# V tiles of two dilations and the combined products kept in DRAM per head pair, in rows of 8 KB

## The chip, the cores and the metric

The kernel runs on one core of a Trainium2 chip. A core has a matrix engine (TensorE, in the profile PE, with its weight loads PEld), a vector engine (DVE), a scalar engine (ACT), GpSimd (POOL) and a queue engine (SP). Each executes its own instructions in order and waits on semaphores for the others. Transfers between DRAM and the on-chip memory (SBUF) are carried out by 16 DMA engines; an instruction of SP, ACT or POOL issues them. The metric is device time in microseconds of one execution, the median of several runs. Before the change it is 2009.21 us.

## The reference

One decoder layer: a projection of `x` (2048 positions x 1024) to queries, keys, values, gates and the inputs of a state-space mixer; causal attention with three dilations; the mixer; a norm for each branch; one output projection; a residual and a layer norm. Cut to the part that the change touches:

```python
DILATIONS = (1, 4, 16)                       # 16 heads of 64, 128 steps back
for o, l in dilation 1, 4, 16: o, l = dilated_window_attention(q, k, v, slopes, dilation)
wts = softmax(stack([l1, l2, l3]))
y_att = wts[0] * o1 + wts[1] * o2 + wts[2] * o3
y_att = rms_norm(y_att * silu(z_att), att_norm_g)
...
mix = concatenate([y_att, y_ssm])
x = layer_norm(alpha * x + mix @ w_out, ln_g, ln_b)
```

In the kernel the heads go in pairs (`pr`, 0 to 7): a pair is one row of 128 channels. The kernel counts the dilations backwards: `d` = 0 is dilation 16, `d` = 1 is 4, `d` = 2 is 1.

## The kernel before, in words

**First stage, about 0 to 1150 us.** The input projection, as fast matrix products of 7 instead of 8 blocks, runs as 37 jobs. PE works through job after job (L260 to L264, L309), while ACT, DVE and POOL prepare the weights of the next one: ACT rounds a block to the high half (L216), POOL or DVE forms the low half (L217). Into this stream are put the convolution, from about 1/3 of the stage, and the 32 units of the state-space mixer, in the last third. The order of PE, DVE, ACT and POOL is that of the program (a manual schedule); `after(n, f)` puts `f` n steps later, a step being one of the 7 products of a job.

Four jobs give the values. `fin_v` (L353) stores them to `d_v[0]`, an array of [16, 128, 1024] floats whose rows, 4 KB each, are one position with all heads. `copy_v(s, b)` (L547), issued by POOL, then makes a second array `d_v[1]` with the positions in the order of dilation 4: for each of the two column halves `s`, 16 copies of 128 rows of 2 KB, from step 95 (first half) and step 254 (second).

**Second stage, attention, about 1150 to 1610 us.** Eight pairs, each with 3 dilations x 4 quarters x 2 halves = 24 units. A unit is: scores on PE (L947), a reduction with the bias table on DVE (L953), exponentials on ACT (L962), transposes on PE (L976, L984) that DVE copies out (L978, L987), and the products with V on PE (L1002). V of one dilation is a tile `v` of 128 partitions x 16 blocks x 128 channels, and, for `d` > 0, a second tile `vs` with the same rows moved by 64. `load_v` (L880) fetches them: `d` = 0 from `d_v[0]` by four POOL transfers; `d` = 1 from `d_v[1]` by POOL; `d` = 2 from `d_v[0]`, for all pairs but the first by SP. In all of these, one row of a transfer is the 128 channels of one pair at one position: 512 bytes. The order of SP's queue is the program's too in this stage.

After the last unit of a pair its softmax statistics are written to `d_st`, gathered again in another layout (`cm`, L1061), and made into the weights of the three dilations by DVE, ACT and POOL (`weights`, L1063). The weights are stored to `d_wd` (L1081) and broadcast to 64 partitions per head (`broadcast`, L1083, tiles `wb`), while PE is already at the next pair. `broadcast` begins, for `d` > 0, with a DVE memset of one element of the tile (L1087). POOL multiplies and adds (`combine`, L1099: L1111, L1115, L1125); the last product, with the gate `zt`, is the tile `u`, the pair's part of the output projection's input. `wb`, `zt` and `u` share one ring of three buffers; five tiles are taken from it per pair, so the `wb` of the third dilation gets the buffer in which the `u` of the pair before that lay. `keep_u` (L1095) stores `u` to `d_ua`, [16, 128, 7, 128], in rows of 512 bytes: for pairs 0 to 5 SP does it two pairs later, at the start of the second dilation, between the broadcasts; for pair 6 ACT does it after attention; pair 7 stays in SBUF.

**Third stage, the output, about 1600 to 2002 us.** For 16 blocks of 128 positions, `fetch_raw` (L1150) loads the attention part from `d_ua` (L1157, one row of 3.5 KB per partition: the seven pairs' channels) and the state-space part from `d_us`; ACT and DVE split it into a high and a low half (`split`, L1159, L1167, L1169); PE multiplies (L1201 to L1203). Pair 7's weights, broadcasts and combination fall into the start of this stage, on DVE.

Of the kernel before, what the change touches and what calls it, by code (L numbers as in the profile page):

```python
# [9 lines left out]
F32 = mybir.dt.float32  # L10
# [7 lines left out]
D = 1024  # L18
# [10 lines left out]
def hybrid_layer(ctx, tc, xb, xc, w52, wv, wdt, convw, convb, dtb, alog, dskp, gcol, wout,  # L29
# [3 lines left out]
    nc = tc.nc  # L33
# [13 lines left out]
    d_za = [dtile(f"d_za{i}", [128, S]) for i in range(8)]  # L47
    d_v = [dtile(f"d_v{d}", [16, 128, D]) for d in range(2)]
    d_wc = dtile("d_wc", [12, 7, 128, 1024])
# [8 lines left out]
    d_wo = dtile("d_wo", [16, 128, 2, D])  # L58
    d_ua = dtile("d_ua", [16, 128, 7, 128])
    d_st = [dtile(f"d_st{i}", [3, 4, S]) for i in range(8)]  # L60
# [10 lines left out]
    with ExitStack() as c1:  # L71
# [281 lines left out]
        def fin_v(s, p):  # L353
            def f(ci, q, b, e):
                for x in range(2):
                    nc.sync.dma_start(dap(d_v[0], 4 * (8 * p + 4 * q + 2 * b + x) * D + 512 * s + 256 * ci,
                                          [[64 * D, 32], [D, 4], [1, 256]]), e[:, 256 * x:256 * x + 256])
            return f
# [188 lines left out]
        def copy_v(s, b):  # L547

            o = (b % 4 * 512 + b // 4 * 16) * D + 512 * s
            nc.gpsimd.dma_start(dap(d_v[1], b * 128 * D + 512 * s, [[16 * D, 8], [D, 16], [1, 512]]),  # L550
                                dap(d_v[0], o, [[64 * D, 8], [D, 16], [1, 512]]))

# [297 lines left out]
    with ExitStack() as c2:  # L850
# [29 lines left out]
        def load_v(A, x, d, queue=nc.gpsimd):  # L880

            o, t, c0 = int(x == "vs"), io.tile([128, 16, 128], F32, name=x, bufs=3), A["pr"] * 128
            A[x][d] = t
            if d == 0:
                for j in range(4):
                    nc.gpsimd.dma_start(t[j:128:4], dap(d_v[0], j * D + c0, [[64 * D, 32], [4 * D, 16], [1, 128]]))
            else:
                queue.dma_start(t[:, 0:16 - o], dap(d_v[d % 2], 64 * o * D + c0,
                                                        [[D, 128], [128 * D, 16 - o], [1, 128]]))

# [204 lines left out]
        def keep_u(A, queue):  # L1095
            queue.dma_start(dap(d_ua, A["pr"] * 128, [[7 * 128, 128], [128 * 7 * 128, 16], [1, 128]]),
                            A["u"].rearrange("p (n t) -> p n t", t=128))

# [51 lines left out]
        def fetch_raw(n, br, u=None):  # L1150
# [5 lines left out]
            else:  # L1156
                queue.dma_start(u[:, 0:7], d_ua[n])  # L1157

# [184 lines left out]
        with tc.manual_schedule(engines={E.PE, E.DVE, E.Activation, E.Pool}):  # L1343
            A = pairs[7]
# [150 lines left out]
```

## Time and profile before

| | us |
|---|---|
| median of 3 runs | 2009.21 (2006.55 to 2010.32) |
| the profiled execution | 2003.82 |
| its span, first to last instruction | 2002.0 |
| PE busy | 1945.7 (97%) |
| DVE, ACT, POOL busy | 1275.8, 1120.0, 998.3 |
| DMA | 447.67 MB in 260656 packets, mean 224 GB/s |
| memset at L1087 waiting for `d_ua<-wb` | 9.4, 4 times |

How to read the profile: a line is written `L947 PE MATMUL S<-k,ex`, the line of the kernel, the engine, the operation, and what it writes from what, by the program's names. "Busy" is time in which an engine has an instruction in execution; the share of the DMA engines is the mean over 16 of them and can pass 1 where packets overlap. A wait is put down to what ended it last. Issues of transfers (`SPq`, `ACTq`, or `DMA_DIRECT2D` on POOL) show how long the issuing engine was held, not how long the transfer took. The granted clock of TensorE was 0.991 in the mean.

### The profile page before, as it was taken

To read this page: it belongs to the slowest core of one execution; us is meant where nothing else is said; L and a number is where in the kernel's file an instruction comes from. 1 tells how busy PE (TensorE), PEld (TensorE's weight loads), DVE (VectorE), ACT (ScalarE), POOL (GpSimd) and SP (SyncE) were. 2 spreads that over 40 slices of the span, in tenths; PEclk is the share of its full clock that TensorE was granted. 3 is DMA by queue.
4 is the path that set the end of the run, shared out by engine and by line. 5 is a ranking of instruction groups with operands and counts; after the bars stand their busy time and mean duration, and the time that the engine had idled before them with its cause. 6 is when DMAs were issued, how large, how long until landed. Compare 5 with 4: busy or idle time off the path is not lost.

```text
span 2002.0 us, 42714 instructions
## 1 busy us (share of the span) xinstructions
PE 1945.7 (97%) x16008; PEld 1588.2 (79%) x16008; DVE 1275.8 (64%) x3204; ACT 1120.0 (56%) x3036; POOL 998.3 (50%) x877
## 2 busy tenths in 40 slices
PE   8999999999999999999999999999999888999998
PEld 7888899888888888988888877777777666888886
DVE  7655376887766655644454388888887736655553
ACT  5454343566556774456566488988888732322220
POOL 0366514666556667155565343676776622432221
PEclk9999999999999999999999999999999998999999
DMA  6788676566787876888888766888888988332210
GB/s 270 236 284 293 213 280 227 159 195 190 237 306 266 279 245 239 312 269 256 272 277 259 256 228 165 229 244 235 252 238 254 265 242 260 134 102 92 92 61 32
DMA packets 260656, 447.67 MB, mean 224 GB/s; under 512 B 44785, under 2 KB 146673, under 8 KB 249057
## 3 DMA queue, kind: packets, MB, share of 16 engines
q1 hardware_dynamic: 170912, 205.39, 32.2%
q0 software_dynamic: 39088, 142.54, 21.6%
q10 hardware_dynamic: 50448, 97.01, 15.7%
q8 instruction: 126, 2.06, 0.4%
q14 instruction: 82, 0.66, 0.1%
HBM read 301.85 MB, written 151.39 MB: 226 GB/s over the span
## 4 chain that ended last, share of the span: by engine, by line
PE 85%; DVE 5%; DMA 4%; ACT 3%; issue 2%; POOL 1%; SPq 0%; ACTq 0%; DVEq 0%; POOLq 0%
PE pp L260 13%; PE pp L264 13%; PE pp L262 13%; PE N L1002 7%; PE S L947 6%; PE T L976 5%; PE pp L309 4%; PE S L1201 4%; PE S L1203 4%; PE S L1202 3%; PE ss L309 2%; PE T L1201 2%; PE T L1203 2%; PE T L1202 2%; PE ss L627 2%
## 5 line engine op out<-in xcount | busy, mean ns | idle before, releaser
L217 POOL TENSOR_TENSOR w<-wr,w 128x512 fp32r<-128x512 f32 x217 | 285.6, 1327 | 268.2 <-ACT w L216 184.0
L962 ACT ACTIVATE P<-P,st 128x192 f32<-128x192 f32 (+1 forms) x768 | 323.4, 423 | 59.9 <-DVE st L953 55.4
L252 ACT COPY ev<-pp 128x512 f32<-128x512 f32 x200 | 117.1, 587 | 315.3 <-PE pp L264 281.5
L953 DVE CUSTOM_DVE_ANT_0 P<-S,tb 128x192 f32<-128x192 f32 (+1 forms) x768 | 205.8, 324 | 53.6 <-PE S L947 44.1
L272 DVE TENSOR_TENSOR ev<-pp,ev 128x512 f32<-128x512 f32 x152 | 101.2, 686 | 140.6 <-PE pp L264 95.9
L216 ACT CAST w<-wr 128x512 fp32r<-128x512 f32 x224 | 134.1, 620 | 23.5 <-DVE wr L211 11.9
L962 ACT ACTIVATION_READ_ACCUMULATOR P<-P,st 128x1 f32 x768 | 145.0, 189 | 0.0
L1111 POOL TENSOR_TENSOR wb<-num,wb 128x2048 f32<-128x2048 f32 x21 | 95.7, 4558 | 93.7 <-DMA wb<-d_wd 90.2
L978 DVE COPY PT<-T 128x512 f32<-128x512 f32 x192 | 131.7, 686 | 3.8 <-PE T L976 3.8
L976 PE MATMUL T<-ident,P 128*128 128x128 f32 x768 | 127.3, 288 | 6.7 <-DVE PT L978 4.5
L1002 PE MATMUL N<-PT,v 128*64 128x64 f32 (+1 forms) x1536 | 124.5, 259 | 4.2 <-DVE PT L978 3.5
L976 PEld LDWEIGHTS T<-ident,P 128*128 128x128 f32 x768 | 81.3, 141 | 52.9 <-ACT P L962 16.8
L211 DVE TENSOR_TENSOR wr<-wr 128x512 f32<-128x512 f32 x128 | 112.2, 877 | 9.3 <-DMA wr<-w 5.9
L947 PE MATMUL S<-k,ex 64*64 64x192 f32 (+1 forms) x2048 | 108.8, 322 | 3.2 <-issue 3.2
L1002 PEld LDWEIGHTS N<-PT,v 128*64 128x64 f32 x1536 | 79.4, 138 | 38.3 <-issue 22.7
L459 DVE SCALAR_TENSOR_TENSOR ss<-U,cw,ss 128x512 f32<-128x512 f32 x144 | 106.0, 752 | 2.9 <-ACT ss L455 0.6
L1177 DVE TENSOR_REDUCE tb<-P 128x128 f32<-128x1024 f32 x30 | 60.2, 2006 | 45.1 <-ACT P L1174 21.1
L1239 POOL TENSOR_TENSOR k<-k,wb 128x1024 f32<-128x1024 f32 x8 | 25.8, 3225 | 122.0 <-DVE k L1238 122.0
L587 ACT ACTIVATE mt<-csb,wdr 128x128 f32<-128x128 f32 x256 | 78.9, 395 | 0.9 <-PE ss L627 0.8
L947 PEld LDWEIGHTS S<-k,ex 64*64 64x64 f32 x2048 | 66.4, 134 | 15.4 <-issue 8.9
L596 DVE TENSOR_TENSOR mt<-mt,ss 128x1024 f32<-128x1024 f32 x32 | 39.0, 1220 | 54.1 <-ACT mt L592 53.7
L260 PE MATMUL pp<-TT4h,w 128*128 128x512 f32 x176 | 69.6, 395 | 0.0
(493 smaller groups left out, 5991.1 us busy)
## 6 DMA issues: line engine op xcount, KB each, us to landing
wr<-w ACTq DMA_DIRECT2D x164, 256.0 KB
d_wc<-w SPq DMA_DIRECT2D x48, 512.0 KB
w<-d_wc POOLq DMA_DIRECT2D x48, 512.0 KB, 6.4
wb<-d_wd SPq DMA_DIRECT2D x48, 512.0 KB
d_wo<-wot POOLq DMA_DIRECT2D x32, 512.0 KB, 4.3
csb<-d_cs ACTq DMA_DIRECT2D x32, 512.0 KB
d_wv<-w SPq DMA_DIRECT2D x14, 1024.0 KB
w<-d_wv POOLq DMA_DIRECT2D x14, 1024.0 KB, 8.7
```

What stands on the lines that cost most here:

```text
L216: nc.scalar.copy(h, r)
L217: low.tensor_tensor(l, r, h.bitcast(F32), op=OP.subtract)
L260: nc.tensor.matmul(ps, w[:, 0, k], th[:, k], start=start and k == 0, stop=False, skip_group_check=not start)
L262: nc.tensor.matmul(ps, w[:, 0, k], tl[:, k], start=False, stop=False, skip_group_check=not start)
L264: nc.tensor.matmul(ps, w[:, 1, k], th[:, k], start=False, stop=(k == 3), skip_group_check=not start)
L309: nc.tensor.matmul(o, (th, tl)[j == 1][:, k, t], w[:, int(j == 2), k], start=start and r % 2 == k == j == 0, stop=(k == 3 and j == 2), ski ...
L947: nc.tensor.matmul(o, A["q"][d][64 * h:64 * h + 64, blk, 64 * a:64 * a + 64], kv, start=True, stop=True)
L953: nc.vector.tensor_tensor_reduce(P[:, h, cs], sp[h][:, cs], t, -0.125, 3.0e38, OP.add, OP.min, accum_out=stat(A, 0, d, h, blk))
L962: nc.scalar.activation(p, p, AF.Exp, bias=stat(A, 0, d, h, blk), scale=-1.0, accum_out=stat(A, 1, d, h, blk))
L976: nc.tensor.transpose(tp[:, h, i], P[:, h, 256 * i:256 * i + 128], ident)
L978: nc.vector.tensor_copy(pt, tp)
L1002: nc.tensor.matmul(o, l, r, start=start, stop=True, skip_group_check=True)
```

## The change

V of dilations 4 and 1 gets arrays of its own, `d_vt[1]` and `d_vt[2]`, each [8 pairs, 128 partitions, 16 blocks, 128 channels]: for a pair exactly what the SBUF tile holds, 8 KB per partition. `copy_v` makes both, with two POOL transfers where there was one. Each moves 512 rows of 512 bytes, for one pair and a quarter of the positions; the steps at which it is called stay. `load_v` reads `v` of `d` > 0 in rows of 8 KB, and `vs` in two halves, by partitions 0 to 63 and 64 to 127, in rows of 7.5 KB. `d` = 0 is read as before. `d_ua` becomes [7 pairs, 128 partitions, 2048]: `keep_u` stores rows of 8 KB, and `fetch_raw` reads seven pieces of 512 bytes per partition.

```diff
-    d_v = [dtile(f"d_v{d}", [16, 128, D]) for d in range(2)]
+    d_v = dtile("d_v", [16, 128, D])
+    d_vt = {d: dtile(f"d_vt{d}", [8, 128, 16, 128]) for d in (1, 2)}
...
-    d_ua = dtile("d_ua", [16, 128, 7, 128])
+    d_ua = dtile("d_ua", [7, 128, 2048])
...
         def copy_v(s, b):
 
-            o = (b % 4 * 512 + b // 4 * 16) * D + 512 * s
-            nc.gpsimd.dma_start(dap(d_v[1], b * 128 * D + 512 * s, [[16 * D, 8], [D, 16], [1, 512]]),
-                                dap(d_v[0], o, [[64 * D, 8], [D, 16], [1, 512]]))
+            pr, n = 4 * s + b // 4, b % 4
+            t, c = pr * 128 * 2048, pr * 128
+            nc.gpsimd.dma_start(dap(d_vt[1], t + n * 512, [[128, 4], [16 * 2048, 8], [2048, 16], [1, 128]]),
+                                dap(d_v, 16 * n * D + c, [[512 * D, 4], [64 * D, 8], [D, 16], [1, 128]]))
+            nc.gpsimd.dma_start(dap(d_vt[2], t + 32 * n * 2048, [[2048, 32], [128, 16], [1, 128]]),
+                                dap(d_v, 32 * n * D + c, [[D, 32], [128 * D, 16], [1, 128]]))
...
         def load_v(A, x, d, queue=nc.gpsimd):
 
-            o, t, c0 = int(x == "vs"), io.tile([128, 16, 128], F32, name=x, bufs=3), A["pr"] * 128
+            t, c0 = io.tile([128, 16, 128], F32, name=x, bufs=3), A["pr"] * 128
             A[x][d] = t
             if d == 0:
                 for j in range(4):
-                    nc.gpsimd.dma_start(t[j:128:4], dap(d_v[0], j * D + c0, [[64 * D, 32], [4 * D, 16], [1, 128]]))
+                    queue.dma_start(t[j:128:4], dap(d_v, j * D + c0, [[64 * D, 32], [4 * D, 16], [1, 128]]))
+            elif x == "v":
+                queue.dma_start(t, d_vt[d][A["pr"]])
             else:
-                queue.dma_start(t[:, 0:16 - o], dap(d_v[d % 2], 64 * o * D + c0,
-                                                        [[D, 128], [128 * D, 16 - o], [1, 128]]))
+                queue.dma_start(t[0:64, 0:15], d_vt[d][A["pr"], 64:128, 0:15])
+                queue.dma_start(t[64:128, 0:15], d_vt[d][A["pr"], 0:64, 1:16])
...
         def keep_u(A, queue):
-            queue.dma_start(dap(d_ua, A["pr"] * 128, [[7 * 128, 128], [128 * 7 * 128, 16], [1, 128]]),
-                            A["u"].rearrange("p (n t) -> p n t", t=128))
+            queue.dma_start(d_ua[A["pr"]], A["u"])
...
-                queue.dma_start(u[:, 0:7], d_ua[n])
+                queue.dma_start(u[:, 0:7], d_ua[:, :, n * 128:n * 128 + 128].rearrange("h p t -> p h t"))
```

No instruction changes its place on PE, DVE and ACT; on SP and POOL only transfers are replaced or added where they stood. Two places show it. The first is SP's queue in attention, from the gather of one pair's statistics to the last broadcast of its weights. `d_st` and `cm` are the statistics, `tb` a bias table, `d_wd` and `wb` the weights. Before:

```order
L1061 DMA cm<-d_st_113 128x6x32
L888 DMA v<-d_v_84 128x16x128
L888 DMA vs<-d_v_84 128x15x128
L878 DMA tb_13450<-tabs 128x2x320
L1081 DMA d_wd_121<-cm 128x3x32
L1089 DMA wb<-d_wd_121 64x2048 x2
L1096 DMA d_ua<-wb 128x16x128
L1089 DMA wb<-d_wd_121 64x2048 x2
L878 DMA tb_13741<-tabs 128x2x128
L1089 DMA wb<-d_wd_121 64x2048 x2
```

And the same place of the changed program:

```order
L1067 DMA cm<-d_st_114 128x6x32
L892 DMA v<-d_vt_86 128x2048
L894 DMA vs<-d_vt_86 64x1920
L895 DMA vs<-d_vt_86 64x1920
L882 DMA tb_13489<-tabs 128x2x320
L1087 DMA d_wd_122<-cm 128x3x32
L1095 DMA wb<-d_wd_122 64x2048 x2
L1102 DMA d_ua<-wb 128x2048
L1095 DMA wb<-d_wd_122 64x2048 x2
L882 DMA tb_13780<-tabs 128x2x128
```

`v` and the store to `d_ua` have 128 rows where they had 2048, `vs` is two transfers of 64 rows where it was one of 1920, and all the rest keeps its place.

The second is POOL's queue in the first stage, around the first two copies; `w` are the halves of the next job's weights, `U` the convolution's input. Before:

```order
L217 TENSOR_TENSOR w<-wr,w 128x512 x5
L550 DMA d_v_85<-d_v_84 128x1x512
L217 TENSOR_TENSOR w<-wr,w 128x512
L437 DMA U<-d_cu_94 128x4x128 x2
L438 DMA U<-d_cu_94 128x127
L439 MEMSET U 128x3
```

And now:

```order
L218 TENSOR_TENSOR w<-wr,w 128x512 x5
L552 DMA d_vt_85<-d_v 4x128x128
L554 DMA d_vt_86<-d_v 512x1x128
L218 TENSOR_TENSOR w<-wr,w 128x512
L438 DMA U<-d_cu_95 128x4x128 x2
L439 DMA U<-d_cu_95 128x127
```

One copy of 128 rows has become two of 512 rows each, ahead of the same weight halves.

More of the change, by code (lines that the diff above doesn't have):

```diff
@@ L355, in f @@
                 for x in range(2):
-                    nc.sync.dma_start(dap(d_v[0], 4 * (8 * p + 4 * q + 2 * b + x) * D + 512 * s + 256 * ci,
+                    nc.sync.dma_start(dap(d_v, 4 * (8 * p + 4 * q + 2 * b + x) * D + 512 * s + 256 * ci,
                                           [[64 * D, 32], [D, 4], [1, 256]]), e[:, 256 * x:256 * x + 256])
```

## The prediction

> **What bounds the kernel now.** I read the page first: the span, and the chain that ended last.
>
> ```profile
> span 2002.0 us, 42714 instructions
> PE 85%; DVE 5%; DMA 4%; ACT 3%; issue 2%; POOL 1%; SPq 0%; ACTq 0%; DVEq 0%; POOLq 0%
> ```
>
> TensorE sets the time, and all DMA waits together hold 4% of the chain. A change that touches only transfers gains where PE idles, so I next read the busy time by stage (columns: the stage, its length, busy us of PE, PEld, DVE, ACT and POOL with instruction counts, granted clock, DMA share, GB/s).
>
> ```profile
> 357.00:520.00 163.00, 163.00 (x721) 134.97 (x720) 127.98 (x192) 101.06 (x179) 104.71 (x113) 1.00 0.66 193
> 860.00:1130.00 270.00, 270.00 (x1530) 225.12 (x1529) 129.51 (x244) 161.94 (x333) 153.46 (x160) 1.00 0.82 264
> 1160.00:1570.00 410.00, 396.48 (x7511) 296.35 (x7511) 347.15 (x1770) 355.83 (x1598) 253.98 (x214) 1.00 0.79 227
> 1570.00:1700.00 130.00, 108.41 (x932) 84.67 (x931) 72.02 (x160) 46.89 (x127) 51.24 (x38) 0.91 0.93 269
> 1700.00:1900.00 200.00, 200.00 (x882) 162.64 (x881) 116.17 (x153) 55.24 (x76) 63.13 (x22) 1.00 0.31 103
> ```
>
> The first two rows hold the copies of V: PE never idles there. In attention (third row) it idles 13.5 us, at the passage to the output (fourth row) 21.6 us, in the output (fifth row) not at all. What this change can win lies in rows three and four. In attention I looked for waits that end on a transfer the change touches. There is one: the memset of one element at L1087, which gives VectorE the buffer of the pair's last weights. This is the view of that line.
>
> ```profile
> L1087 DVE MEMSET wb<- x14: 59/59/59, 1230.7 to 1576.8; 128x1 f32 x14
>   DMA d_ua<-wb: 9.4, 4
> ```
>
> That buffer held `u` of two pairs before, so the memset waits until `keep_u` has landed. It is tiny, but VectorE runs in order, and behind it stand the next scores' reductions, which ScalarE and then PE wait for. The five stalls in time order, from the timeline of VectorE (start, us, what; in brackets the idle time before it and who ended it):
>
> ```profile
> 1350.05 0.06 DVE L1087 MEMSET wb<- 128x1 f32 x1 [1.94 <-PE N L1002]
> 1406.63 0.06 DVE L1087 MEMSET wb<- 128x1 f32 x1 [2.42 <-DMA d_ua<-wb]
> 1462.63 0.06 DVE L1087 MEMSET wb<- 128x1 f32 x1 [1.93 <-DMA d_ua<-wb]
> 1519.35 0.06 DVE L1087 MEMSET wb<- 128x1 f32 x1 [2.61 <-DMA d_ua<-wb]
> 1576.76 0.06 DVE L1087 MEMSET wb<- 128x1 f32 x1 [2.44 <-DMA d_ua<-wb]
> ```
>
> And the busy time around each, with the columns of the stages above:
>
> ```profile
> 1348.00:1352.00 4.00, 2.68 (x63) 1.98 (x55) 2.00 (x12) 1.75 (x9) 3.49 (x2) 1.00 1.08 258
> 1404.00:1412.00 8.00, 6.26 (x128) 4.76 (x122) 5.11 (x27) 4.80 (x22) 4.83 (x3) 1.00 1.09 257
> 1460.00:1468.00 8.00, 6.77 (x152) 5.21 (x146) 5.59 (x28) 5.28 (x24) 4.58 (x3) 1.00 1.09 254
> 1516.00:1524.00 8.00, 6.64 (x108) 4.95 (x103) 3.96 (x22) 4.05 (x17) 4.66 (x2) 0.79 1.11 269
> 1572.00:1580.00 8.00, 6.40 (x134) 5.01 (x130) 5.32 (x30) 5.18 (x23) 5.07 (x2) 1.00 1.10 282
> ```
>
> VectorE stands 1.94 + 2.42 + 1.93 + 2.61 + 2.44 = 11.34 us; PE idles 1.32 + 1.74 + 1.23 + 1.36 + 1.60 = 7.25 us in the five windows, and around the fourth its clock is 0.79, which costs another 8 x 0.21 = 1.7 us. The first stall is put down to PE, but PE itself stood there for VectorE; I count it with the others.
>
> **The change, part by part.** First the price of a byte by its row length. The rows are: 512-byte rows on SP's queue (only V loads ran), 8 KB rows being read (`q`), 8 KB rows being stored (`d_wv`, SP), and one of the old copies from DRAM to DRAM.
>
> ```profile
> 1388.00:1392.00 4.00, 2.85 (x45) 2.02 (x48) 3.72 (x21) 3.77 (x19) 1.71 (x6) 1.00 1.12 331
> 1418.00:1420.00 2.00, 2.00 (x45) 1.53 (x44) 1.48 (x7) 1.86 (x7) 2.00 (x1) 1.00 1.01 402
> 24.00:25.50 1.50, 1.50 (x10) 1.05 (x9) 1.50 (x2) 0.44 (x1) 0.00 (x0) 1.00 1.00 421
> 359.00:360.50 1.50, 1.50 (x8) 1.27 (x7) 1.01 (x3) 0.97 (x2) 0.57 (x1) 1.00 0.36 145
> ```
>
> So a store of 1.05 MB costs 3.2 us in rows of 512 bytes (331 GB/s) and 2.5 us in rows of 8 KB (421): 0.7 us less. Loading `v` and `vs`, 2.03 MB, costs 6.1 us at 331 and 5.05 us at 402: 1.1 us less. [...]
>
> *Attention, SP's queue.* Two pieces of SP's timeline (start, us of issue), an early pair whose V was long in and a later one:
>
> ```profile
> 1225.42 0.36 SPq L1081 DMA_DIRECT2D d_wd<-cm  x1
> 1227.50 4.43 SPq L1089 DMA_DIRECT2D wb<-d_wd  x4
> ...
> 1384.79 0.54 SPq L888 DMA_DIRECT2D v<-d_v  x1
> 1385.41 2.02 SPq L888 DMA_DIRECT2D vs<-d_v  x1
> 1387.53 2.86 SPq L878 DMA_DIRECT2D tb<-tabs  x1
> 1391.91 0.36 SPq L1081 DMA_DIRECT2D d_wd<-cm  x1
> 1395.32 1.13 SPq L1089 DMA_DIRECT2D wb<-d_wd  x2
> 1396.50 0.59 SPq L1096 DMA_DIRECT2D d_ua<-wb  x1
> 1397.20 5.82 SPq L1089 DMA_DIRECT2D wb<-d_wd  x2
> ```
>
> The store of `u` goes behind a broadcast of weights, which waits for the write of `d_wd`, which goes behind `v`, `vs` and a table. `d_wd` takes 3.4 us (1391.91 to 1395.32) where V is still moving and 2.1 us where it is not (1225.42 to 1227.50), so at most 1.3 us is queueing; V is done 1.1 us sooner, and I take that. With 0.7 us of its own, `u` lands 1.8 us sooner. Taking 1.8 us (or all of it) from each stall leaves 0.14 + 0.62 + 0.13 + 0.81 + 0.64 = 2.34 of 11.34 us, so 79% goes. PE gains 0.79 x 7.25 = **5.7 us**. Of the lowered clock I take half, **0.9 us** (another stall as long, at 1404, did not lower it). Bounds: nothing, and all 9.0 us. What is late next is ScalarE, 356 of 410 us busy, so PE's other idle time stays. The extra DMA per `vs` costs SP some 0.5 us of issue in a queue that stood 2.02 + 2.86 us for room; SP still reaches `d_wd` in time, since that waits for POOL's weights. `wb` for the next dilations, the table and the gather behind `keep_u` move forward with it, and POOL, which waits for `wb`, with them.
>
> *The passage to the output.* PE's longest wait lies here, on `num` of the output's second factor, which VectorE forms after the last pair's weights came (rows of the timelines of SP, ACT, DVE and PE):
>
> ```profile
> 1624.60 0.38 SPq L1081 DMA_DIRECT2D d_wd<-cm  x1
> 1633.60 9.47 SPq L1089 DMA_DIRECT2D wb<-d_wd  x6
> ...
> 1624.80 8.36 ACTq L1392 DMA_DIRECT2D num<-d_za  x1
> ...
> 1653.74 2.29 DVE L1111 TENSOR_TENSOR wb<-num,wb 128x2048 f32<-128x2048 f32 x1 [4.64 <-DMA wb<-d_wd]
> ...
> 1659.55 0.80 PE L1203 MATMUL S<-k,num 128*128 128x512 f32 x1 [12.04 <-DVE num L1169]
> ```
>
> The DMA engines are nearly full in this stage (share 0.93 from 1570 to 1700): weights, residuals, `u` of pair 6, `z`, and six broadcasts. The change takes 0.7 us of work out of it. And ACT's queue, held 8.36 us behind the 2048 short rows of `u`, is free sooner, so that the last residuals are read earlier, beside fewer broadcasts. I take **2 us** of the 12; ends: 3 us slower (the 128-byte rows of `d_wd` alternating with 8 KB rows) and 8 us faster (as long as ACT's queue stood).
>
> *The output stage.* Rows of `u` are now read as 7 pieces of 512 bytes per partition: 0.46 MB at 331 GB/s is 1.4 us against 1.1 us at 402. Most of the sixteen loads lie in the last stage, with a DMA share of 0.31 and a PE that never idles, and they are asked for two steps ahead: 0. If PE waited for all, 16 x 0.3 = 5 us.
>
> *The copies.* 32 copies become 64, and move 16.8 MB for 8.4. POOL's issue rows:
>
> ```profile
> L886 POOL DMA_DIRECT2D v<-d_v x32 | 21.0, 663 | 19.2 <-PE N L1002 10.2 <-PE pp L264 7.3 <-issue 1.7
> L550 POOL DMA_DIRECT2D d_v<-d_v x32 | 20.7, 646 | 0.0
> L888 POOL DMA_DIRECT2D v<-d_v x9 | 10.7, 1193 | 16.5 <-PE N L1002 16.5
> ```
>
> A new copy has 512 rows, as an L886 load has, so 64 x 0.66 = 42 us of issue for 20.7: 21 us more, in stages where POOL is idle 58 us (163 - 104.7) and 117 us (270 - 153.5). Behind a copy on POOL stand the low halves of the next job's weights, wanted a job later. Taken as 0; uncovered, it is 21 us. In attention POOL's `v` (2048 rows, 1193 ns) falls to about the 646 ns of L550's 128 rows, off the path: 0.
>
> **Sum**: 5.7 + 0.9 + 2 = 8.6 us off the profiled 2003.8 us gives 1995.2. The median of the three runs shown is 5.4 us above that execution, so against 2009.2: 2000.6 us, in its own range of 1992 (9.0 + 8) to 2008.
>
> **Rivals.** *(1) Short rows cost nothing.* If the 331 GB/s is the price of contention (writes of weights run in the same window), not of row length, `u` lands when it did and all stalls stay: 2009 us, give or take 2. Against it: the share of that window is 1.12, so engines were kept busy by fewer bytes. [...] *(2) The wait moves.* ScalarE or the statistics gather, which also stops VectorE, takes the place of the memset; PE gets back a third, and the passage nothing: 2009.2 - 2.2 = 2007 us. For it: ACT is 87% busy in attention; against it: 7.25 of PE's 13.5 us of idle time in the stage lie in the five windows of the memset. *(3) Slower: the copies crowd a few DMA engines.* The old copy, whose outermost count is 8, moved 145 GB/s at a share of 0.36 although nothing else ran, so it used only part of the engines. The new one for dilation 4 has an outermost count of 4. At half the rate 0.26 MB takes 3.6 us instead of 1.8 us, 16 times in the 270 us from 860 on, where the mean share is 0.82: 0.82 + 16 x 3.6 / 270 = 1.03 on those engines. From a share of 1 on, loads of the state-space units and weights fall behind, and PE, in order, stands behind them. If each of the 16 costs PE 1.8 us: 2000.6 + 28.8 = 2029 us. [...] Against the rival: PE is 270.00 of 270 us busy in that stretch, and its inputs are fetched a job ahead. *(4) It does not do what it says*: the built program's rows are 8 KB as written, so no chance.
>
> **Chances.** Forecast 0.66, (1) 0.10, (2) 0.12, (3) 0.12. A difference under 0.2%, 4 us, is about what a measurement of this kernel can't tell from none. The forecast's range lies mostly beyond it (0.62 faster, 0.04 within); (2) is split evenly; (1) is within, (3) slower: faster 0.68, same 0.20, slower 0.12. The range leaves out (3) and the edges: 1991 to 2010.
>
> **What would show it.** Right: the memset waits less than 0.9 us on `d_ua` in each pair, `d_wd` to `wb` falls to about 2.3 us, PE's idle time from 1160 to 1570 from 13.5 to about 8 us, PE's wait at the passage from 12 to about 10 us. Wrong: `keep_u` landing when it did, waits of PE between 357 and 1130 us, or PE waiting on `P<-d_ua` after 1700.

## The result and the profile after

| | before | after |
|---|---|---|
| median | 2008.66 us, 4 runs (2006.55 to 2010.32) | 2027.74 us, 4 runs (2024.66 to 2028.50) |
| profiled execution | 2003.82 | 2027.90 |

The ratio is 1.0093, with a 95% interval of 1.0075 to 1.011: slower by 0.9%, where 0.4% faster was forecast. The page's span and its chain that ended last:

```profile
span 2026.1 us, 42777 instructions
PE 61%; DMA 6%; DVE 3%; issue 2%; ACT 2%; POOL 1%; SPq 1%; ACTq 0%; POOLq 0%; DVEq 0%
```

By stage, with the columns of the prediction's table. The last row is one stretch over all copies of V.

```profile
357.00:520.00 163.00, 159.58 (x700) 130.76 (x699) 137.89 (x185) 98.71 (x173) 116.99 (x121) 1.00 0.74 202
860.00:1130.00 270.00, 264.59 (x1481) 219.49 (x1480) 125.27 (x236) 160.71 (x332) 168.38 (x170) 0.99 0.86 273
1160.00:1570.00 410.00, 387.82 (x7142) 287.91 (x7140) 326.62 (x1674) 337.94 (x1517) 239.29 (x216) 0.98 0.80 221
1570.00:1700.00 130.00, 112.59 (x1286) 85.55 (x1279) 81.80 (x268) 66.70 (x236) 66.31 (x57) 0.92 0.90 263
357.00:1130.00 773.00, 762.37 (x4052) 636.99 (x4051) 483.38 (x754) 464.91 (x900) 479.58 (x461) 1.00 0.81 259
```

And the same stretch of the kernel before:

```profile
357.00:1130.00 773.00, 770.31 (x4112) 646.43 (x4111) 470.37 (x762) 468.18 (x904) 446.05 (x435) 1.00 0.77 252
```

PE, which hardly idled beside the copies, now loses 770.31 - 762.37 = 7.9 us there; in attention it idles 22.2 us where it idled 13.5, at a lower granted clock (0.98 against 1.00). The memset on which the forecast rested now reads so:

```profile
L1093 DVE MEMSET wb<- x14: 59/59/59, 1241.1 to 1604.4; 128x1 f32 x14
  DMA d_ua<-wb: 17.1, 5
```

The waits were to shrink by 79%; they grew from 9.4 to 17.1 us. This line also gives a ruler, used for every run below: its first start, its last start and the span cut the program in three. Before: 1230.7, then 346.1 to 1576.8 (**attention's way**), then 425.2 to the end. After: 1241.1, 363.3, 421.7. So 10.4 us were lost ahead of attention, 17.2 in it, and 3.5 won behind it: 24.1 us, the whole difference of the two spans. Such a cut is of one execution; in five kernels whose first stage is the same (before, e2_u_only, f1_before_halves, h1_split_blocks, h2_split_even_odd below) the first start came between 1227.4 and 1230.7, so some 3 us of this part are chance, and the other parts may hold as much or more. The execution profiled before was also a quick one: its 2003.82 us lie below all four runs of the table, while the one after lies at its median. The medians differ by 19.1 us, so some 5 of the 24.1 are chance. PE's busy time beside the copies is steadier: 770.2 to 771.0 us in the five kernels, 762.4 to 763.7 in three that share the first stage of the change (after, e1_vs_whole, f4_two_queues).

What stands ahead of the store of `u` on SP's queue shows the loss in attention (start, us of issue):

```profile
1464.72 0.53 SPq L892 DMA_DIRECT2D v<-d_vt  x1
1465.36 0.48 SPq L894 DMA_DIRECT2D vs<-d_vt  x1
1465.90 0.59 SPq L895 DMA_DIRECT2D vs<-d_vt  x1
1466.54 0.65 SPq L882 DMA_DIRECT2D tb<-tabs  x1
1471.61 0.37 SPq L1087 DMA_DIRECT2D d_wd<-cm  x1
1476.91 1.09 SPq L1095 DMA_DIRECT2D wb<-d_wd  x2
1478.05 0.58 SPq L1102 DMA_DIRECT2D d_ua<-wb  x1
```

From `d_wd` to the first `wb` it is 5.3 us, not 2.3 as forecast and not 3.4 as before (3.7 to 5.4 over the seven pairs in attention, 2.1 to 3.9 before). Two windows of this pair, the first while only `v` moves, the second while only the two halves of `vs` move (the last column is GB/s):

```profile
1467.00:1468.50 1.50, 1.01 (x20) 0.60 (x12) 1.47 (x11) 0.98 (x5) 0.39 (x1) 1.00 1.02 410
1469.50:1472.50 3.00, 3.00 (x48) 2.07 (x47) 2.73 (x15) 2.77 (x14) 1.28 (x4) 1.00 1.00 248
```

`v` in rows of 8 KB moves at 410 GB/s, as forecast. `vs` in rows of 7680 bytes moves at 248, with the engines just as busy (share 1.00): slower than the short rows it replaced (331 in the prediction's row). That is the first theory, **half tiles**: a transfer into partitions 0 to 63 or 64 to 127 alone is slow.

Ahead of attention, the waits from 357 to 520 us (us in total, times, longest) hold two kinds on the convolution's output `co` that were not among those of before, and POOL's issues of the copies are longer than forecast:

```profile
ACT co L467 <- DVE ss L460: 24.8, 13, 4.8
ACT co L467 <- DMA d_xs<-co: 20.9, 6, 6.1
...
L552 POOL DMA_DIRECT2D d_vt<-d_v x32 | 38.6, 1207 | 0.4 <-issue 0.4
L554 POOL DMA_DIRECT2D d_vt<-d_v x32 | 23.4, 730 | 0.0
```

The copies hold POOL 38.6 + 23.4 = 62.0 us, not 42 (before: 20.7). VectorE's 24 small copies for the convolution, beside POOL's work, lengthened too:

```profile
L445 DVE COPY U<-U 128x127 f32<-128x127 f32 x24 | 27.8, 1177 | 0.0
```

They took 13.3 us before (L444). But of the 7.9 us only 3.4 are lost from 357 to 520 us; 5.4 are lost from 860 to 1130, behind the convolution, beside the second half of the copies. What PE waited for there (it waited for nothing before):

```profile
PE pp L261 <- ACT xdeh L603: 3.5, 1, 3.5
PE pp L261 <- DMA w<-d_wc: 1.9, 2, 1.6
```

The weights `w<-d_wc` landed 7.5 us after their issue in the median there, against 6.7 before. Two theories stood for this stretch: **POOL's time** in the issues, and **the copies' packets** on the DMA engines, the third rival of the prediction.

### The profile page after: what moved, and what is told of

Its sections match the earlier page's. It is cut to its first block, busy times and chain, and to the rows that moved or that the text cites. A ratio compares the mean times of both kernels' runs of the same rounds, so it can differ in the third digit from the quotient of the medians.

```text
span 2026.1 us, 42777 instructions
## 1 busy us (share of the span) xinstructions
PE 1956.5 (97%) x16008; PEld 1592.9 (79%) x16008; DVE 1288.8 (64%) x3204; ACT 1117.7 (55%) x3036; POOL 1030.8 (51%) x918
## 4 chain that ended last, share of the span: by engine, by line
PE 61%; DMA 6%; DVE 3%; issue 2%; ACT 2%; POOL 1%; SPq 1%; ACTq 0%; POOLq 0%; DVEq 0%
PE pp L261 8%; PE pp L265 7%; PE pp L263 7%; PE N L1008 6%; PE S L953 5%; PE T L982 4%; PE S L1206 4%; PE S L1208 3%; PE S L1207 3%; PE T L1206 2%; PE T L1208 2%; PE T L1207 2%; PE ss L631 1%; PE ss L622 1%; PE T L990 1%
## 5 line engine op out<-in xcount | busy, mean ns | idle before, releaser
L982 PE MATMUL T<-ident,P 128*128 128x128 f32 x768 | 129.7, 293 | 10.9 <-DVE PT L984 8.4
L212 DVE TENSOR_TENSOR wr<-wr 128x512 f32<-128x512 f32 x128 | 116.8, 913 | 8.0 <-DMA wr<-w 4.3
L953 PEld LDWEIGHTS S<-k,ex 64*64 64x64 f32 x2048 | 67.7, 136 | 19.5 <-issue 13.3
L261 PE MATMUL pp<-TT3h,w 128*128 128x512 f32 x176 | 70.6, 401 | 8.6 <-ACT xdeh L603 3.5
```

The costliest lines, as they stand in the source:

```text
L261: nc.tensor.matmul(ps, w[:, 0, k], th[:, k], start=start and k == 0, stop=False, skip_group_check=not start)
L953: nc.tensor.matmul(o, A["q"][d][64 * h:64 * h + 64, blk, 64 * a:64 * a + 64], kv, start=True, stop=True)
L982: nc.tensor.transpose(tp[:, h, i], P[:, h, 256 * i:256 * i + 128], ident)
```

## The experiments

Each run has a kernel of before beside it on the same chip, whose median was 2005.2 to 2008.5 us; ratios are against that. Where an expectation says dilation 1 or dilation 2, it means the kernel's `d` = 1 (dilation 4) or `d` = 2 (dilation 1).

### vs in one transfer

```diff
-                queue.dma_start(t[0:64, 0:15], d_vt[d][A["pr"], 64:128, 0:15])
-                queue.dma_start(t[64:128, 0:15], d_vt[d][A["pr"], 0:64, 1:16])
+                queue.dma_start(t[:, 0:15], d_vt[d][A["pr"], :, 0:15])
```

> The changed kernel, but the shifted tile vs is filled by one transfer of 128 partitions (rows of 7680 B) in place of two of 64 partitions. It reads unshifted rows, so the terms of the shifted blocks get wrong values; all instructions and bytes stay. Theory 'half tiles' (a transfer into 64 partitions moves at about half the rate of one into 128, 218 to 246 against up to 434 GB/s in the changed kernel's trace, and so the factors' broadcast and the store of u behind it land later than before): vs then moves at 400 GB/s or more, the five waits of the memset L1092 for the store of u fall from 17.1 us to under 4, and the time falls by 12 to 18 us against the changed kernel's 2027.7, to 2010 to 2016. Rival 'the eight-KB rows themselves crowd the queue': nothing changes in rate, the waits stay near 17 us and the time within 3 us of 2027.7. In both, the ten us lost ahead of 1140 us stay.

Measured: 2006.9 us, ratio 1.0005 (0.9986 to 1.0024), shorter than was expected (2010 to 2016). The tile holds unshifted rows here: the kernel leaves the shift out. The memset, a window with `vs` alone, and the stretches of attention and of the copies:

```profile
L1092 DVE MEMSET wb<- x14: 59/59/59, 1239.5 to 1578.2; 128x1 f32 x14
  DMA d_ua<-wb: 2.0, 3
...
1452.50:1454.50 2.00, 2.00 (x36) 1.44 (x36) 2.00 (x13) 2.00 (x12) 0.32 (x1) 1.00 1.02 428
...
1160.00:1570.00 410.00, 400.52 (x7528) 297.97 (x7517) 346.84 (x1783) 359.58 (x1620) 249.60 (x225) 1.00 0.76 232
357.00:1130.00 773.00, 762.60 (x4056) 637.75 (x4055) 481.77 (x755) 466.76 (x901) 479.12 (x460) 1.00 0.81 260
```

The same bytes in the same rows move at 428 GB/s instead of 248, the waits all but go, attention's way is 338.7 us instead of 363.3, and some 18 us of the median come back. The loss ahead of attention stays, as both theories on it said (762.6 against 762.4). So, in these executions, long rows win 7.4 us in attention by the ruler, and the halves cost 24.6. The 24.6 is an upper end: the execution profiled here, 2000.3 us, was the second shortest of twelve (1998.2 to 2017.6). By the medians the halves cost 18 us in this run and 21 in the next.

### The halves alone, on the kernel before

```diff
+                for a in ((0, 64), (64, 128)) if o else ((0, 128),):
+                    queue.dma_start(t[a[0]:a[1], 0:16 - o], dap(d_v[d % 2], (64 * o + a[0]) * D + c0,
+                                                            [[D, a[1] - a[0]], [128 * D, 16 - o], [1, 128]]))
```

> The kernel before, with one thing of the change alone: the shifted tile vs is filled by two transfers, into partitions 0 to 63 and 64 to 127, in place of one into 128. Rows stay at 512 B, bytes and layout stay, the result is the same. Theory 'half tiles': each half moves at a lower rate, the broadcasts and the store of u behind it on SP's queue land later, the memset's waits for the store of u at L1089 rise from 9.4 us to 13 to 20, the way from the first to the last of these memsets grows from 346 us to 352 to 365, and the time is 8 to 20 us over before. Rival 'halves cost only with rows of 7680 B': waits at 9 to 11 us, the time within 3 us of before.

Measured: 2027.3 us, ratio 1.0105 (1.009 to 1.0121), more than was expected. The memset and a window with a half of `vs`:

```profile
L1088 DVE MEMSET wb<- x14: 59/59/59, 1230.5 to 1602.0; 128x1 f32 x14
  DMA d_ua<-wb: 27.8, 6
...
1463.50:1465.00 1.50, 1.50 (x24) 1.15 (x24) 1.23 (x9) 1.28 (x7) 0.73 (x3) 1.00 1.17 201
```

This one edit, with no new copy, no long row and no new layout, costs as much as the whole change. It is the cause in attention. It halves `vs` of both `d` = 1 and `d` = 2; e4_one_copy below, in which only `d` = 1 stays halved, takes as long as a kernel without halves (e2_u_only).

### Why a half is slow: its number, its size or its place

Two runs split `vs` in two transfers again, on the kernel before. The first splits by blocks, each transfer going into all 128 partitions:

```diff
+                for n in ((0, 8), (8, 15)) if o else ((0, 16),):
+                    queue.dma_start(t[:, n[0]:n[1]], dap(d_v[d % 2], (64 * o + 128 * n[0]) * D + c0,
+                                                         [[D, 128], [128 * D, n[1] - n[0]], [1, 128]]))
```

> The kernel before, with vs filled by two transfers again (as in f1_before_halves), but each goes into all 128 partitions: blocks 0 to 7, then blocks 8 to 14. Theory 'half tiles by partitions' (a transfer that reaches only partitions 0 to 63 or 64 to 127 is slow): nothing is lost, the memset's waits stay at 7 to 12 us, the way from its first to its last stays at 344 to 352 us, the time within 4 us of before. Rival 'two transfers in place of one cost it, by their number or their halved size': waits of 20 us or more, a way of 365 us or more, the time 15 to 25 us over before, as with f1_before_halves.

The second takes the even partitions and then the odd ones, 64 each:

```diff
+                for a in (0, 1) if o else (None,):
+                    queue.dma_start(t[:, 0:16 - o] if a is None else t[a:128:2, 0:15],
```

> The kernel before, with vs filled by two transfers into 64 partitions each, but the even and then the odd partitions of all 128. Theory 'half tiles by place' (it matters that the 64 partitions lie in one half of the tile, so that a part of the ways into SBUF stands idle): as before, waits of 7 to 12 us, the time within 4 us of before. Theory 'half tiles by count' (64 partitions are slow wherever they lie): the time 15 to 25 us over before, waits of 20 us or more.

Measured: 2002.6 us, ratio 0.997 (0.9957 to 0.9982), and 2003.5 us, ratio 0.9971 (0.996 to 0.9982). A window with `vs` of the first, and of the second:

```profile
1443.50:1445.00 1.50, 1.25 (x24) 0.94 (x24) 1.50 (x11) 1.50 (x9) 0.39 (x1) 1.00 1.13 342
```

```profile
1448.00:1450.50 2.50, 1.93 (x29) 1.36 (x28) 2.27 (x11) 2.50 (x15) 0.88 (x3) 1.00 1.11 328
```

342 and 328 GB/s, against 201 for the halves of the tile, with the same number of transfers and, in the second, 64 partitions in each as well. The memset's waits are 10.5 and 6.0 us, attention's way 347.2 and 350.7. It is the place that counts: 64 partitions in one half of the tile at 201 GB/s, 64 spread over all of it at 328. Why the place counts is not shown; the ways into SBUF of which the last expectation speaks were the author's guess. That both splits are even a little faster than before was not expected; see below.

### The two halves from two queues

```diff
+                q2 = nc.scalar if queue is nc.sync else queue
-                queue.dma_start(t[64:128, 0:15], d_vt[d][A["pr"], 0:64, 1:16])
+                q2.dma_start(t[64:128, 0:15], d_vt[d][A["pr"], 0:64, 1:16])
```

> The changed kernel, with the upper half of dilation 2's vs issued by ScalarE's queue and the lower half by SP's as before, so that both halves can be under way at once. If a half tile is slow because it reaches only a part of what 128 partitions reach, and two halves at once reach all, the waits of the memset L1094 for the store of u fall from 17.1 to under 8 us and the time to 2010 to 2018. If the halves serialize whatever queue issues them, the waits stay at 14 to 20 us and the time at 2024 to 2030. ScalarE's issue costs 0.4 us a pair on an engine that is 85% busy there, 2 us in all at most.

Measured: 2026.5 us, ratio 1.0098 (1.0079 to 1.0117). The memset, and when ScalarE and SP issued their halves of one pair:

```profile
  DMA d_ua<-wb: 14.2, 6
...
1458.21 0.49 ACTq L896 DMA_DIRECT2D vs<-d_vt  x1
...
1465.74 0.48 SPq L894 DMA_DIRECT2D vs<-d_vt  x1
```

Nothing came back, but ScalarE issued its half 7.5 us ahead of SP, so the halves were hardly under way at once. Whether two at once would be quick is not answered.

### u alone

The kernel before with `d_ua` as [7, 128, 2048], `keep_u` in rows of 8 KB and the fetch in seven pieces, as in the change's diff; V as before.

> The kernel before with only the products' part of the change: u kept in rows of 8 KB per pair, fetched in 512 B pieces behind; V's copies and loads as before. My prediction's own step, alone: the store of u is 0.7 us sooner, of which the memset waits keep the rest, so the 9.4 us of waits of L1087 fall to 5 to 7, attention gains 2 to 4 us, the passage behind it 2, and the time is 2003 to 2006 against 2008.7 (faster by 0.1 to 0.3%). Rival 'fetching u back in 512 B pieces costs what the store gains': within 2 us of 2008.7. Rival 'the loss of the change is in u': 2018 or more.

Measured: 2007.9 us, ratio 1.0009 (0.9995 to 1.0022).

```profile
L1087 DVE MEMSET wb<- x14: 59/59/59, 1227.4 to 1584.5; 128x1 f32 x14
  DMA d_ua<-wb: 8.0, 4
```

The waits fell by 1.4 us, and attention's way was 357.1 us against 346.1, at a granted clock of 0.98 against 1.00, while the stretch behind it took 422.7 us against 425.2. The expected gain of 0.1 to 0.3% lies outside the interval.

### Without the second copy

```diff
-            nc.gpsimd.dma_start(dap(d_vt[2], t + 32 * n * 2048, [[2048, 32], [128, 16], [1, 128]]),
-                                dap(d_v, 32 * n * D + c, [[D, 32], [128 * D, 16], [1, 128]]))
...
+            elif d == 2:
+                o = int(x == "vs")
+                queue.dma_start(t[:, 0:16 - o], dap(d_v, 64 * o * D + c0, [[D, 128], [128 * D, 16 - o], [1, 128]]))
```

> The changed kernel without the second copy (d_vt[2]): 32 copies with four outermost pieces stay for dilation 1, and dilation 2's V and shifted V are loaded from d_v in rows of 512 B as before, each in one transfer of 128 partitions. Theory 'half tiles': attention's waits at the memset for the store of u fall below 9 us, since both loads are whole again and u's store is in long rows, which gives back 10 to 16 us in attention. Theory 'POOL's issue' and theory 'the copies' packets' both give back a part of the ten us ahead of 1140 us: with 32 issues of 1.2 us in place of 61.7 us of issues some 6 us by the first; by the second, where the four-piece copies are the crowding ones, 0 to 3 us. Time 2004 to 2015; above 2022 would speak against all three.

Measured: 2007.2 us, ratio 1.001 (0.9997 to 1.0022). The stretch of the copies, the memset, and two microseconds in which only one copy of four outermost pieces moves:

```profile
357.00:1130.00 773.00, 770.95 (x4119) 646.38 (x4119) 474.49 (x764) 467.26 (x904) 464.30 (x435) 1.00 0.78 252
...
L1094 DVE MEMSET wb<- x14: 59/59/59, 1231.0 to 1587.1; 128x1 f32 x14
  DMA d_ua<-wb: 14.6, 6
...
359.50:361.50 2.00, 2.00 (x10) 1.65 (x10) 1.00 (x4) 1.64 (x3) 1.24 (x1) 1.00 0.32 71
```

The time is within what was expected; the waits of the memset, 14.6 us, are not (below 9). The expectation took both loads of `vs` for whole, but this kernel fills `vs` of `d` = 1 still in two halves, from POOL's queue; only `d` = 2 is whole. Whether these halves make the longer waits was not tried; attention's way is 356.1 us, no longer than with `u` alone (357.1), where no load is halved. The four-piece copy does move slowly, 71 GB/s at a share of 0.32, where the old one moved 145 at 0.36. But alone, and with POOL 18.3 us busier than before in the whole stretch, it costs PE nothing (770.95).

### The copies from SP's queue

In `copy_v`, `nc.gpsimd` becomes `nc.sync`, twice.

> The changed kernel, but the 64 copies of V in DRAM are issued by SP's queue in place of POOL's; bytes and pieces are the same. Theory 'POOL's issue' (issuing the copies takes POOL 1.2 and 0.7 us each, 61.7 us in all against 20.7 before; POOL then runs back to back, and VectorE's small copies at L445, 24 of them, last until POOL's run ends, 27.8 us between 357 and 700 us against 13.3 before): L445 falls to 10 to 13 us, PE's busy time between 357 and 520 us returns from 159.6 to 162 to 163, and the time falls by 7 to 11 us, to 2017 to 2021. Theory 'the copies' packets' (the copies occupy few DMA engines and the store of co lands late, so ScalarE waits 20.9 us for it): the wait for d_xs<-co stays at 15 us or more, PE's busy time there stays below 160.5, and the time stays within 4 us of 2027.7, or grows, since SP's queue holds the stores behind copies that wait for V.

Measured: 2063.3 us, ratio 1.0284 (1.0259 to 1.0308). VectorE's small copies fell as expected, to 13.1 us, and `co` waited no longer for its store. But SP reached the copies much earlier than POOL had (the first at 34.9 us, against 357.1 with the change) and then held its stores behind them; from 200 to 357 us, where no copy had run, PE lost 8.2 us:

```profile
L445 DVE COPY U<-U 128x127 f32<-128x127 f32 x24 | 13.1, 565 | 0.0
...
200.00:357.00 157.00, 148.45 (x939) 133.34 (x939) 85.38 (x105) 58.11 (x92) 55.00 (x49) 0.97 0.75 261
```

The copies no longer lay beside the convolution, so this run does not tell the two theories apart.

### The first copies behind the convolution

```diff
-                later.setdefault(95 + 4 * j, []).append(lambda j=j: copy_v(0, j))
+                later.setdefault(170 + 5 * j, []).append(lambda j=j: copy_v(0, j))
```

> The changed kernel, with the first 32 copies issued behind the convolution (steps 170 to 245 in place of 95 to 155; the last 32 stay). If the convolution is what they disturb, by POOL's time or by their packets, the way of co's writes returns to 213 us, the waits of ScalarE for d_xs<-co and for VectorE before co fall from 53 us to under 5, PE's busy time from 357 to 520 us is 162.5 to 163, and 3 to 6 us come back: 2021 to 2025. If the copies only shift their cost, the same time is lost between 600 and 860 us and the time stays at 2027 within 2.

Measured: 2033.2 us, ratio 1.014 (1.0121 to 1.0159), longer than either expectation had it. The convolution is free again, and the loss has moved behind it, larger (the changed kernel's PE has 258.20 us in the second row's stretch):

```profile
357.00:520.00 163.00, 163.00 (x721) 135.04 (x719) 126.86 (x192) 101.30 (x180) 95.05 (x96) 1.00 0.57 169
600.00:860.00 260.00, 252.21 (x1474) 215.20 (x1475) 162.75 (x241) 157.63 (x307) 168.12 (x150) 0.99 0.87 292
```

### POOL held as long, without the second copy's packets

The kernel is the one with one copy, e4_one_copy, with six memsets in the place of each second copy.

```diff
+        idle = late.tile([128, 16], F32, name="idle")
...
+            for _ in range(6):
+                nc.gpsimd.memset(idle, 0.0)
```

> The kernel with one copy (run e4_one_copy: no d_vt[2], dilation 2 loaded from d_v), and in place of each second copy six small memsets on POOL, some 0.75 us: the second copy's time on POOL without its packets. Theory 'POOL's time': the way from the first to the last of the convolution's writes of co (L467 there 212.9 us with one copy, 217.6 with two) grows to 216 or more, VectorE's copies at L445 rise from 16.4 to 22 us or more, and PE's busy time between 357 and 520 us falls from 163.0 to 161 or less. Theory 'the copies' packets': all three stay as with one copy (213, 17 us, 163.0). Time: with the first theory 2011 to 2017, with the second 2005 to 2010.

Measured: 2009.9 us, ratio 1.0023 (1.0008 to 1.0038).

```profile
357.00:1130.00 773.00, 765.88 (x4075) 641.72 (x4074) 482.03 (x756) 468.43 (x904) 480.70 (x618) 1.00 0.78 251
```

POOL is as busy as with the change (480.7 against 479.6), and PE loses 770.95 - 765.88 = 5.1 us against the run with one copy, without a byte more. `co` waits for its store again (20.9 us over the run). The small copies at L445 stay at 14.7 us, so their lengthening isn't needed for it. Yet the time lies where the packets' theory put it (2005 to 2010), and PE's busy time from 357 to 520 us, 162.1, between the two theories (161 or less, 163.0). The profiled execution, 2016.5 us, was also the second longest of nine; the median lies only 2.7 us above that of e4_one_copy, and the intervals of the two ratios overlap. So the run speaks for POOL's time, but does not settle it.

### A version that keeps the gain

The two costs can be left out: `d` = 1 as before (its old copy takes POOL 0.64 us, not 1.2), and for `d` = 2 a third part of 64 rows a pair, shifted by a block, so that `vs` is one transfer. `u` is kept in long rows.

```diff
+    d_vt = dtile("d_vt", [8, 192, 16, 128])
...
+        def copy_vs(pr):
+            nc.gpsimd.dma_start(d_vt[pr, 128:192, 0:15], d_vt[pr, 0:64, 1:16])
...
+                if d == 2:
+                    src = d_vt[A["pr"], 64 * o:64 * o + 128, 0:16 - o]
```

> A version meant to keep the gain and drop the two costs. For dilation 2 alone, V in DRAM as it lies in SBUF, 192 rows a pair: rows 0 to 63, 64 to 127, and rows 0 to 63 once more, shifted by a block (one copy of 480 KB in rows of 7680 B a pair, 8 in all), so that vs is one transfer of 128 partitions in rows of 7680 B. Dilation 1 as before (its copies take POOL 0.65 us each, not 1.2); u as in the change. By my theories: attention as in e1_vs_whole, or a few us longer since dilation 1 stays in rows of 512 B: from the first to the last memset 338 to 348 us against 346 before; the stretch ahead of the first memset 1231 to 1236 us against 1230.7 before and 1241.1 with the change, POOL's issues being 43.7 us in place of 61.7; time 1998 to 2006, up to 0.4% faster than before. It falls if the first memset comes after 1238 us.

Measured: 2004.0 us, ratio 0.9982 (0.997 to 0.9994): faster than both kernels, by 0.2% and 1.1%.

```profile
L1100 DVE MEMSET wb<- x14: 59/59/59, 1229.2 to 1576.3; 128x1 f32 x14
  DMA d_ua<-wb: 2.4, 2
...
1160.00:1570.00 410.00, 395.72 (x7480) 295.61 (x7478) 344.90 (x1762) 354.74 (x1596) 251.00 (x209) 1.00 0.74 224
PE S L960 <- issue: 9.5, 6, 2.7
...
357.00:1130.00 773.00, 771.04 (x4124) 647.13 (x4122) 473.50 (x764) 466.97 (x904) 472.93 (x476) 1.00 0.81 267
```

Nothing is lost ahead of attention, though the DMA engines are as busy as with the change (0.81) and move more (267 GB/s against 259). So more packets alone do not make the loss either. The weights `w<-d_wc` land as early as before (6.7 us in the median from 860 to 1130 us).

In attention the waits of the memset all but went, but PE idles 410 - 395.72 = 14.3 us, no less than before's 13.5. From 1230 to 1580 us its waits for VectorE's copies `PT` fell from 9.1 to 0.9 us; its waits without a releaser in the profile ("issue") rose from 4.0 to 13.4, of which the fence shows the larger line. So PE stands as long, at other waits. What ends them is not known, nor whether the change brings them: they are 9.0 us in e1_vs_whole, where the waits for `PT` are 1.1, and 5.5 and 12.3 in h1_split_blocks and h2_split_even_odd, whose rows are as short as before.

### That version, with POOL held longer

Five memsets of the same kind at each step of the copies.

> The version g2_whole_vs, with five small memsets on POOL at each step of the copies (some 0.57 us), so that POOL is as long held there as by the change (42.1 + 18 = 60 us against 61.7), with g2's packets. Theory 'POOL's time': PE's busy time from 357 to 1130 us falls from 771.0 to 764 to 767 (the change 762.4; memsets beside one copy, f2_pool_busy, 765.9), ScalarE waits again for d_xs<-co (15 us or more), and the time grows by 4 to 7 us over g2_whole_vs, to 2007 to 2011. If the four-piece copy itself is needed for the loss, PE stays at 770 or more and the time within 2 us of g2_whole_vs.

Measured: 2003.5 us, ratio 0.9974 (0.9954 to 0.9994).

```profile
357.00:1130.00 773.00, 769.35 (x4114) 645.12 (x4113) 477.70 (x763) 468.83 (x904) 487.76 (x629) 1.00 0.81 267
```

POOL is busier than with the change, PE loses 1.7 us of the expected 4 to 7, and the time is that of g2_whole_vs. POOL's time by itself falls as the theory.

### u as before, and vs split, on that version

> The version g2_whole_vs, but with u kept as before (rows of 512 B in d_ua, fetched whole behind). My prediction put 0.7 us a pair on the store of u in rows of 8 KB; run e2_u_only found nothing of it with the slow V loads ahead. If the term is real once V is quick: the memset's waits rise from 2.4 us to 5 to 9, and the time by 2 to 4 us, to 2006 to 2008 (ratio 1.000 against 0.998). If the store in long rows is worth nothing, or the fetches in 512 B pieces give it back: the waits may rise, the time stays within 1.5 us of g2_whole_vs or falls.

> The version g2_whole_vs, with vs in two transfers by blocks as in h1_split_blocks (for dilation 2 rows of 4096 and 3584 B, each into 128 partitions). If the split by blocks is worth 0.3% by itself, as h1_split_blocks had it beside before, the time is 1996 to 2001 (ratio 0.995 to 0.997). If that gain and the one of whole rows are the same one (the queue ahead of the broadcasts), the time stays at 2002 to 2006.

Measured: 2002.2 us, ratio 0.997 (0.9957 to 0.9984), and 2003.0 us, ratio 0.9972 (0.9959 to 0.9985). In the first the memset's waits rise to 4.3 us, and the time does not: the long rows of `u` are worth nothing here either. In the second no further gain of the split shows: its interval overlaps that of g2_whole_vs.

## Why the prediction was wrong, by its steps

- **"V is done 1.1 us sooner"** is the step that failed in attention. It priced `v` and both halves of `vs` at the 402 GB/s of a read of 8 KB rows into 128 partitions (`q`). `v` moved at 410. The halves of `vs` moved at 248, so that `d_wd` took 5.3 us to its broadcast in place of 2.3; with `vs` whole (e1_vs_whole) it took 1.7 to 2.4, as forecast. The diff showed partitions 0 to 63 and 64 to 127, and the prediction priced of them only an issue of 0.5 us; that they could cost in rate was among no rival. f1_before_halves shows this edit alone at +1.05%, h1_split_blocks and h2_split_even_odd that the place of the partitions makes it.
- **"u lands 0.7 us sooner"**, from 331 against 421 GB/s, gained nothing in any run: alone (1.0009) or with quick V loads (0.9982 with it, 0.997 without). With it and V of `d` = 2 in short rows, attention's way was 357.1 and 356.1 us in two kernels (e2_u_only, e4_one_copy) against 346.1 before, at a granted clock of 0.98 in both against 1.00 from 1160 to 1570 us. By these two figures the clock would make some 8 of the 10 to 11 us (an estimate, 410 x 0.02); why it was lower is not settled.
- **"79% of the stalls go"** is right for the memset once `vs` is whole: its waits fall from 9.4 to 2.0 us (e1_vs_whole) and 2.4 (g2_whole_vs), as good as the forecast's 79%. What the forecast made of it, **"PE gains 0.79 x 7.25 = 5.7 us"**, is not borne out. PE's idle time in attention, which was to fall from 13.5 to about 8 us, fell to 9.5 in e1_vs_whole and was 14.3 in g2_whole_vs, where it stood at "issue" instead. That has the form of rival (2), the wait moves, though not to ScalarE or the gather. The way shrinks by 7.4 us in e1_vs_whole, against a forecast of 6.6, and not at all in g2_whole_vs (347.1 us), so how much of the 7.4 us belongs to the waits stays open.
- **The passage to the output**, 2 us: right. PE's wait there fell from 12.04 to 8.81 us, the stretch behind the last memset by 3.5 us, and ScalarE's issue of `num` from 8.36 to 0.44 us, as the prediction had it. Other kernels agree: with `u` in short rows this wait of PE is 10.5 to 12.0 us in five (11.2 in the mean), with long rows 8.2 to 10.9 in ten (9.3).

```profile
1683.59 0.79 PE L1208 MATMUL S<-k,num 128*128 128x512 f32 x1 [8.81 <-DVE num L1174]
```

- **"The copies: taken as 0"** failed by 7.9 us of PE's time and 10.4 us by the ruler; waits of PE between 357 and 1130 us were named as a sign of being wrong, and came. An issue of the four-piece copy was taken as 0.66 us from a load of 512 rows, and took 1.2. But the runs do not let POOL's time stand as the cause by itself: with the four-piece copy it cost PE 5.1 us in one execution (f2_pool_busy), without it 1.7 (m1_busy_on_g2).
- **Rival (3)** gave the right time, 2029 us, by luck: it put 29 us on the copies, of which 10 are there. Its mechanism is half borne out. The halved rate that its sum took is there, 71 GB/s (e4_one_copy) against the old copy's 145. How many engines a copy uses no run shows, only their shares, 0.32 and 0.36; nor does one show the 1.8 us of PE that the sum took for each copy. The four-piece copy is present in every run that lost much in that stretch; alone it lost nothing (PE's 770.95 us in e4_one_copy against 770.31 before), and in these runs the loss came with something beside it, the second copy or a busier POOL. That PE stood behind weights landing late was seen for 1.9 us. Which trait of the copy matters, the low rate or the long issue (1.2 us), stays open: a kernel with eight outermost pieces in place of four (m2_eight_pieces), meant to tell them apart, gave no measurement.
- **The range** was narrower than its own terms. With nothing won in attention and 3 us lost at the passage, its slow end would be 2009.2 + 3 = 2012 us in place of 2008; the 2027.74 measured lie beyond that too. No run shows the 3 us that it allowed for rows of 128 bytes alternating with rows of 8 KB; the stretch behind the last memset got 3.5 us shorter.

So of +24.1 us in the profiled executions, the halves make +24.6, the long rows -7.4, the copies +10.4, and the stretch behind -3.5, each with a few us of chance. Of the medians' +19.1 the halves make 18 (e1_vs_whole) to 21 (f1_before_halves), and all the rest together about nothing (1.0005, 0.9986 to 1.0024).

## What to carry to other kernels

Price a transfer by the partitions that it touches as well as by its row length: here a tile filled by its two halves (248 GB/s, against 428 whole) lost 18 us by the medians and 24.6 by the ruler, more than the 7.4 us that rows sixteen times as long won, and a copy that makes the tile whole in DRAM (8 transfers of 480 KB in g2_whole_vs, 0.51 to 0.59 us of POOL's issue each, with PE's busy time beside the copies at 771.0 us against 770.3 before) was far cheaper than the halves. When a diff splits a transfer, look for a row of a transfer of that shape; the trace of before held one all along, the broadcasts of `wb` into 64 partitions each, in a window with four of them and nothing else on SP's queue:

```profile
1229.00:1231.50 2.50, 2.50 (x35) 1.70 (x33) 2.44 (x16) 2.50 (x12) 0.00 (x0) 1.00 0.92 223
```

223 GB/s in rows of 8 KB at a share of 0.92 lies near the 201 and 248 that the halves then moved, though a broadcast reads one row for all its partitions and a half does not. And follow a shorter wait to the engine that sets the time: here the memset's waits went, and PE's idle time in one kernel did not.

## What the runs showed of the hardware that was not expected

- A transfer into partitions 0 to 63 or 64 to 127 moved 201 GB/s in rows of 512 bytes (f1_before_halves) and 248 in rows of 7680 (the change), at a share of the engines of 1.0 or more. Into 64 even partitions it moved 328 in rows of 512 bytes (h2_split_even_odd), into all 128 partitions 342 in rows of 512 bytes (h1_split_blocks) and 428 in rows of 7680 (e1_vs_whole).
- Splitting `vs` in two transfers that reach the whole tile made the kernel 0.3% faster than one transfer (0.997 in h1_split_blocks and 0.9971 in h2_split_even_odd, both intervals below 0.9983). No run explains it; on top of the long rows no further gain shows (k2_whole_and_split).
- A copy from DRAM to DRAM with four outermost pieces of 512-byte rows took POOL 1.2 us to issue (the change, L552), one with 32 pieces and as many rows 0.7 us (L554), and the old one with 128 rows 0.65 us (before, L550).
